# Half 1's x staged in one go, its roots spread together, the sums of x on one engine and the roots one stretch later, in a hybrid attention and retention kernel

## The chip, the cores and the metric

One core of a Trainium2 chip runs the whole program. The metric is the device time of one execution in microseconds; the number given for a kernel is the median of its runs.

## The reference

One layer of a streaming encoder, for 2048 frames of a new stream (the prompt) and 64 frames of a running one (the sample), all in fp32. Every frame is normalised and goes through one wide projection; its columns are the inputs of a differential attention and of a retention, with gates; both results are projected, merged by the gates, projected again and added to x.

```python
h = rmsnorm(x, norm_g) @ w_in                     # 1024 -> 6144
qa, ka, va, za, qb, kb, vb, zb, ga, gb = split(h)
qa, ka = rmsnorm(qa, qn_g), rmsnorm(ka, kn_g)
oa = diff_attention(qa, ka, va, lam, slopes)      # 4 heads, block-causal, ALiBi
ob = retention(qb, kb * 128 ** -0.5, vb, log_g)   # 4 heads, chunks of 64
oa = rmsnorm(oa, subln_g) * 0.2 * silu(za)
ob = rmsnorm(ob) * silu(zb)
y = x + (sigmoid(ga + b0) * (oa @ w_oa) + sigmoid(gb + b1) * (ob @ w_ob)) @ w_out
```

`rmsnorm` divides each row by the root of its mean square plus 1e-6. The sample's attention also reads 4096 cached keys and values. The normalised keys, the values and the final retention states are outputs too.

## The kernel before

Every fp32 factor is split in a high part of type fp32r and the rest (`hi`, `lo`, or `xh`/`xl` and `wh`/`wl`), and a product is three matmuls: high by high, high by rest, rest by high. The high part is an ACT copy, the rest a subtraction on DVE or POOL.

**The work** is written by a planner in Python. Generators (tasks) emit instructions and yield a time or a condition; the loop runs the task of the lowest priority number whose time has come. The planner keeps a clock for each engine (`self.pe`, `self.act`, `self.dve`, `self.pool`, and `self.dma` for loads) and adds an estimate for each instruction. Buffers are counted by tags: `take` waits for one, `give` returns it with the time from which it is free; `either` takes from the tag that is free first. `self.ar` is an arena of columns, 7104 wide until the prompt's attention starts: `grab` takes stretches of it, `drop` returns them. PE, ACT and DVE execute in the order in which the tasks emit. The instructions of POOL and the DMA issues, all of them on SP, are put in order by the framework.

**The order.** The projection runs as a stream of weight columns (`w_stream`, priority 9) over half 0 (frames 0 to 1023 and the sample), then over half 1 (1024 to 2047). x of a half lies transposed in SBUF as `xh` and `xl`, in two segments of 512 frames. Half 0 begins with three groups of columns in natural layout, va, k and q (`natural`; 128 frames and 512 columns a bank, banks `mm`, of which there are two), then vb (`late`: the second segment first), then q, k of the retention and the gates by Strassen products of seven instead of eight (`strassen`): their left factors are blocks of x and sums of blocks, S1, S2, S4 and a third that replaces a block. `x_sums` (priority 1) forms the sums. For each of four c it adds `xh` and `xl` of two blocks again (`pool_sum` on POOL, L735; `raw_sum` on DVE, L739), adds or subtracts and splits the result (`s_split`, L753 and L756). S1 is formed in the stretch of k, S2, S4 and the third from the end of q on, when their room is free; the third goes back into segment 1 of x once vb has read it.

**The sample's attention** (`sample_attn`, priority 4) starts when the sample's q, k and v are stored, and is woven into half 0's products. It holds 2816 columns of the arena (`held`) and up to four stretches of 1024 for scores. At its end four small matmuls by `fold` (L1768) form its output, the held columns are dropped, and `rms_t` normalises it with the bank `tp`, of which there is one, and one buffer each of `ath` and `atl` (two exist).

**Half 1's x** is normalised in two steps. `x_roots` (spawned after k) loads each of the eight tiles of 128 frames into a stretch of 1024, and `x_root` squares and sums it on ACT (L402), with a reciprocal root on ACT and DVE (L406 to L416); the eight results are columns of `self.roots`. After the first unit of gb, three units before half 0 ends, `x_scaled` and `x_split` start. `x_stage` loads x transposed, in four parts of 256 frames, each two tiles of 128 x 1024: parts 0, 1 and 3 in the arena, part 2 in the two `V` buffers, which the sample uses for its values. For each part `x_scaled` multiplies the unit matrix by the roots (DVE, L449), spreads them over all partitions by matmuls with a matrix of ones (L457, bank `tp`), copies the bank (ACT, L460) and scales x by them and by the norm's gain (DVE, L467, eight of 128 x 256). `x_split` waits until half 0 has read a segment for the last time (`seg_free`, set in the last Strassen unit), and splits each part: four copies on ACT (L499) and four subtractions on DVE (L501).

**The passage.** Half 1 starts with va's first 256 columns: four groups of 256 frames, each of which needs its part's split (`xt_ready`). A group ends in `fin_va`: ACT copies the bank to `thi` (L1245) and `ev` (L1247), DVE subtracts into `tlo` (L1249), and three stores follow. There is one `thi` buffer, there are two of `tlo` and three of `ev`. k and q go through `fin_qk`, with transposes (L1201) into `tp` and `thi` again (L1211 or L1216). `attn_zone` waits until half 0 is done and all eight `xt_ready` are there; it closes the pool that held arena, `V`, `S` and `ath`, opens the attention's pool in its place, and loads at once `dnear`, the keys (`K`), queries (`q`), `dfar` and values (`V`) of two heads and the retention's tables and first blocks, 32 DMAs. The attention of half 0's frames then runs at a higher priority than half 1's projection: scores (L1514, L1515, banks `s` and `tp`), their evacuation on DVE (L1523), the exponential on ACT (L1554), and so on.

Of the kernel before, what the change touches and what calls it, by code (L numbers as in the profile page):

```python
# [8 lines left out]
F32 = mybir.dt.float32  # L9
# [3 lines left out]
ALU = mybir.AluOpType  # L13
# [28 lines left out]
PACE = 700.0  # L42
# [93 lines left out]
class Hybrid:  # L136
# [283 lines left out]

    def x_stage(self):
        for p in range(4):
            if p == 2:
                yield from self.take("V", 2)
                xT = [self.sb(self.ap, [128, 1024], "V", "xT") for _ in range(2)]
            else:
                xT = [span.ap for span in (yield from self.stage(p))]
            t0 = 1024 + 256 * p
            for k in range(2):
                tx = self.ld(xT[k].rearrange("p (c t) -> p c t", c=4),  # L430
                             self.i["x_prompt_T"][512 * k:512 * k + 512, t0:t0 + 256]
                             .rearrange("(c p) t -> p c t", p=128), 1 << 19)
            self.xstaged.append((xT, tx))
            yield self.pe

    def x_scaled(self):


        nc = self.nc
        self.xstaged = []  # L440
        self.spawn(self.x_stage(), 1, "w")
        for p in range(4):
            yield lambda: len(self.xstaged) > p
            xT, tx = self.xstaged[p]
            span = yield from self.grab(256)
            dp = span.ap
            yield lambda: len(self.rooted) >= 8
            for u in range(2):
                nc.vector.tensor_scalar(dp[:, 128 * u:128 * u + 128], self.ident,  # L449
                                        self.roots[:, 2 * p + u:2 * p + u + 1], None, op0=ALU.mult)  # L450
                t = self.V(128, self.pe)
            yield max(t, tx)
            yield from self.take("tp")
            rb = self.psum("tp")[:, :256]
            for u in range(2):
                usl = slice(128 * u, 128 * u + 128)
                nc.tensor.matmul(rb[:, usl], self.ones, dp[:, usl], start=True, stop=True)  # L457
                t = self.P(512)
            yield t
            nc.scalar.copy(dp, rb)  # L460
            t = self.A(256, t)
            self.give("tp", t)
            yield t
            for k in range(2):
                for c in range(4):
                    xc = xT[k][:, 256 * c:256 * c + 256]
                    nc.vector.scalar_tensor_tensor(out=xc, in0=xc, scalar=self.gT[:, 4 * k + c:4 * k + c + 1],  # L467
                                                   in1=dp, op0=ALU.mult, op1=ALU.mult)
                    t = self.V(300, t)
                    yield self.dve - PACE  # L470
            self.xscaled.append((xT, t))
            self.drop(span, t)

    def stage(self, p):
        self.staged[p] = yield from self.grab(1024, 1024)
# [2 lines left out]
    def x_split(self):  # L478
        nc = self.nc
        for p in range(4):  # L480
            seg, col = p // 2, 256 * (p % 2)
            yield lambda: len(self.xscaled) > p
            xT, t = self.xscaled[p]
            if p % 2 == 0:
                yield lambda: self.seg_free[seg] is not None
                yield self.seg_free[seg]
                self.seg_free[seg] = None
                self.x_alloc(seg)
                if seg:
                    for k, x in enumerate((self.xh, self.xl)):  # L490
                        ts = self.ld(x[1][:, :, 512:576].bitcast(F32), self.xkeep[:, :, 64 * k:64 * k + 64], 1 << 18)
            yield t
            for k in range(2):
                for c in range(0, 4, 2):
                    ks = slice(4 * k + c, 4 * k + c + 2)
                    hi = self.xh[seg][:, ks, col:col + 256]
                    lo = self.xl[seg][:, ks, col:col + 256]
                    xk = xT[k][:, 256 * c:256 * c + 512].rearrange("p (c t) -> p c t", c=2)
                    nc.scalar.copy(hi, xk)  # L499
                    t2 = self.A(512, self.pe)  # L500
                    nc.vector.tensor_sub(lo, xk, hi.bitcast(F32))  # L501
                    t2 = self.V(612, t2)
                if p == 2:
                    self.give("V", t2)
                else:
                    self.drop(self.staged[p][k], t2)
                yield self.act - PACE
            self.xt_ready += [t2, t2]
# [222 lines left out]
                self.give(r[3], t, 3)  # L731
        yield self.pe

    def pool_sum(self, out, h, l):
        self.nc.gpsimd.tensor_add(out, h.bitcast(F32), l.bitcast(F32))  # L735
        self.tpool = self.G(512, self.pe)

    def raw_sum(self, out, h, l, t):
        self.nc.vector.tensor_add(out, h.bitcast(F32), l.bitcast(F32))  # L739
        return self.V(512, t)  # L740
# [22 lines left out]
    def x_sums(self):  # L763
        nc = self.nc
        yield lambda: len(self.xt_ready) > 8
        yield self.xt_ready[8]
        yield from self.s_room("S1")
        (a11, a12, a21, a22) = (self.x_block(k) for k in range(4))
        for c in range(4):
            r = yield from self.grab(1024)  # L770
            r0, r1 = r[:, 0:512], r[:, 512:1024]
            self.raw_sum(r0, a21[0][:, c], a21[1][:, c], self.pe)
            self.pool_sum(r1, a22[0][:, c], a22[1][:, c])
            yield self.tpool
            nc.vector.tensor_add(r0, r0, r1)
            t = self.V(512)
            yield from self.s_split("S1", c, r0, t)
            self.drop(r, self.dve + LAT)
        yield from self.s_room("S2")
        yield from self.s_room("S4")  # L780
        third, r, r2 = yield from self.grab(2048, 1024, 1024)
        for c in range(4):
            r0, r1, r3, r4 = r[:, 0:512], r[:, 512:1024], r2[:, 0:512], r2[:, 512:1024]
            d = third[:, 512 * c:512 * c + 512]
            self.pool_sum(r1, a11[0][:, c], a11[1][:, c])
            t1 = self.tpool
            self.pool_sum(r4, a21[0][:, c], a21[1][:, c])
            self.raw_sum(r0, *(s[c // 2][:, c % 2] for s in self.S["S1"]), self.pe)
            self.raw_sum(r3, a12[0][:, c], a12[1][:, c], self.pe)
            yield t1  # L790
            nc.vector.tensor_sub(r0, r0, r1)
            t = self.V(512)
            nc.vector.tensor_sub(r3, r3, r0)
            t2 = self.V(512)
            yield from self.s_split("S2", c, r0, t)
            yield from self.s_split("S4", c, r3, t2)
            yield self.tpool
            nc.vector.tensor_sub(d, r1, r4)
            t3 = self.V(512)
            yield self.dve - PACE  # L800
        self.formed = self.dve + LAT
        self.drop(r, self.formed)
        self.drop(r2, self.formed)
        yield lambda: self.seg1_read is not None
        yield max(t3, self.seg1_read)
        done = []
        for c in range(4):
            nc.scalar.copy(a21[0][:, c], third[:, 512 * c:512 * c + 512])
            done.append(self.A(512, self.pe))
        for c in range(4):  # L810
            yield done[c]
            nc.vector.tensor_sub(a21[1][:, c], third[:, 512 * c:512 * c + 512], a21[0][:, c].bitcast(F32))
            self.s3_ready = self.V(512, done[c])
        self.drop(third, self.s3_ready)
        self.summed = True
# [841 lines left out]
    def sample_attn(self):  # L1657
        nc = self.nc
# [108 lines left out]
        for h in range(4):  # L1767
            nc.tensor.matmul(fp[:, 64 * h:64 * h + 64], oall[:, 128 * h:128 * h + 128], self.fold[:, :64],  # L1768
                             start=True, stop=True)
            t = self.P(512)  # L1770
        for span in held:
            self.drop(span, t)
        o, leave = yield from self.rms_t(fp, 256, self.gsub, t, "pv")
        for h in range(4):
            t = self.put(self.oaT[h], o[:, 64 * h:64 * h + 64], T, 64, True)
# [817 lines left out]
    def w_stream(self):  # L2593
# [51 lines left out]
        for half in range(2):  # L2645
            for k, (c0, f, *_) in enumerate(seqs[half]):
                if c0 is None:
                    self.spawn(self.mark(f"{f}{half}"), 0)
                else:
                    yield from f(half)  # L2650
                if half == 0 and k == 1:
                    self.spawn(self.x_roots(), 2, "w")
                if half == 0 and k == len(seqs[0]) - 1:
                    self.done.add("half0")
                    self.marks["half0"] = self.pe
                if half == 0 and k == len(seqs[0]) - 4:
                    self.xt_ready = []
                    self.spawn(self.x_scaled(), 1, "w")
                    self.spawn(self.x_split(), 1, "w")
# [165 lines left out]
```

## Time and profile before

| what | value |
|---|---|
| median of three runs | 1930.66 us (1928.85 to 1931.25) |
| the profiled execution's own time | 1928.47 us |
| its span, first to last instruction | 1926.5 us |
| mean granted TensorE clock | 0.994 of full speed |
| busy: PE, DVE, ACT, POOL | 98%, 67%, 49%, 31% |

The profile is one execution; its page gives busy times, costliest groups and DMA queues, and its trace answers questions by line, tile or stretch of time. In the timeline a row is start, duration, engine, line, operation, output and inputs, and, in brackets, the idle time before it and what ended it. A busy PE is not PE at its peak, since matmuls overlap; the granted clock tells when it ran at half rate.

### The profile page before, as it was taken

What the parts mean: (1) busy time and instruction counts of PE and PEld (TensorE: products, weight loads), DVE (VectorE), ACT (ScalarE), POOL (GpSimd) and SP (SyncE); (2) the same over time, 40 slices, a digit from 0 to 9 for tenths busy, and PEclk for the clock granted to TensorE, in tenths of its full rate; (3) what the DMA queues carried; (4) which work ended last, traced back from release to release, by engine and by line L of the source; (5) the groups of instructions that cost most, each with busy time, mean ns of one, the idle gap of its engine ahead of it and who ended that gap; (6) DMA issues with size and microseconds to landing.
All of it is one profiled execution on the core that took longest, in us unless ns stands there. A gap on an engine that the chain in (4) does not pass through costs nothing. (4 is left out here: it accounts for less than half of the span.)

```text
span 1926.5 us, 33600 instructions
## 1 busy us (share of the span) xinstructions
PE 1896.9 (98%) x11690; PEld 1696.0 (88%) x11690; DVE 1283.2 (67%) x3046; ACT 949.6 (49%) x2153; POOL 598.7 (31%) x569
## 2 busy tenths in 40 slices
PE   9999999999998999999999999999999999999999
PEld 7777888888877999999999899999999999999887
DVE  6666656665655688856576655558677359997664
ACT  6444445454433456555455555456556455554221
POOL 2520455555652111211211112120211245532442
PEclk9999999999999999999999999999999999999999
DMA  7664356565645867454433643362441488886542
GB/s 249 211 211 131 115 159 189 173 172 172 201 146 167 243 178 210 136 162 136 133 101 108 190 113 103 107 160 84 126 114 38 138 245 261 250 250 209 181 153 77
DMA packets 361323, 313.10 MB, mean 163 GB/s; under 512 B 67905, under 2 KB 319937, under 8 KB 361154
## 3 DMA queue, kind: packets, MB, share of 16 engines
q1 hardware_dynamic: 361154, 310.97, 55.0%
q8 instruction: 92, 1.51, 0.3%
q14 instruction: 77, 0.63, 0.1%
HBM read 205.43 MB, written 104.60 MB: 161 GB/s over the span
## 5 line engine op out<-in xcount | busy, mean ns | idle before, releaser
L961 POOL TENSOR_TENSOR wl<-ws,wh 128x512 fp32r<-128x512 f32 x125 | 171.8, 1387 | 412.8 <-ACT wh L951 326.2
L997 PE MATMUL mm<-xh,wh 128*128 128x512 f32 (+2 forms) x768 | 257.3, 335 | 0.0
L997 PE MATMUL mm<-wh,xh 128*128 128x256 f32 (+1 forms) x760 | 251.4, 331 | 4.7 <-ACT raw L1166 3.0
L997 PE MATMUL mm<-xh,wl 128*128 128x512 f32 (+2 forms) x768 | 251.6, 328 | 0.0
L997 PE MATMUL mm<-xl,wh 128*128 128x512 f32 (+2 forms) x768 | 251.5, 327 | 0.0
L997 PE MATMUL mm<-wh,xl 128*128 128x256 f32 (+1 forms) x760 | 245.2, 323 | 0.3 <-DVE xl L501 0.3
L997 PE MATMUL mm<-wl,xh 128*128 128x256 f32 (+1 forms) x760 | 244.7, 322 | 0.0
L1641 DVE TENSOR_TENSOR atl<-at,ath 128x512 fp32r<-128x512 f32 (+1 forms) x144 | 93.9, 660 | 126.4 <-ACT ath L1639 125.5
L997 PEld LDWEIGHTS mm<-wh,xh 128*128 128x128 f32 x760 | 147.2, 194 | 16.5 <-ACT raw L1166 3.6
L1554 ACT ACTIVATE row<-row,a_mx 128x896 f32<-128x896 f32 (+5 forms) x144 | 149.5, 1041 | 19.6 <-DVE a_mx L1533 19.4
L997 PEld LDWEIGHTS mm<-wl,xh 128*128 128x128 f32 x760 | 147.3, 194 | 10.9
L997 PEld LDWEIGHTS mm<-wh,xl 128*128 128x128 f32 x760 | 146.6, 193 | 11.4 <-DVE xl L501 0.5
L997 PEld LDWEIGHTS mm<-xh,wh 128*128 128x128 f32 x768 | 145.0, 189 | 10.7
L997 PEld LDWEIGHTS mm<-xl,wh 128*128 128x128 f32 x768 | 145.2, 189 | 10.3
L997 PEld LDWEIGHTS mm<-xh,wl 128*128 128x128 f32 x768 | 144.8, 189 | 10.6
L1639 ACT CAST ath<-at 128x512 fp32r<-128x512 f32 (+1 forms) x144 | 79.6, 563 | 138.0 <-PE at L1626 136.0
L1523 DVE CUSTOM_DVE_ANT_0 row<-s,dfar 128x512 f32<-128x512 f32 (+2 forms) x146 | 90.5, 636 | 44.9 <-PE s L1515 38.4
L1398 POOL TENSOR_TENSOR r_y<-r_y,r_sq 128x256 f32<-128x256 f32 x32 | 26.8, 838 | 298.0 <-DVE r_sq L1395 173.1
L1514 PE MATMUL s<-K,q 128*128 128x512 f32 (+3 forms) x242 | 91.6, 380 | 7.0 <-DMA q<-qT 5.2
L1576 DVE SCALAR_TENSOR_TENSOR row<-row,a_w 128x896 f32<-128x896 f32 (+6 forms) x88 | 97.5, 1121 | 0.0
L951 ACT CAST wh<-ws 128x512 fp32r<-128x512 f32 x128 | 77.2, 619 | 35.2 <-PE mm L997 15.9
L721 POOL TENSOR_TENSOR wl<-ws,wh 128x256 fp32r<-128x256 f32 x64 | 55.3, 864 | 121.8 <-ACT wh L712 113.7
(489 smaller groups left out, 5475.5 us busy)
## 6 DMA issues: line engine op xcount, KB each, us to landing
ws<-in_w_in_dram SPq DMA_DIRECT2D x160, 256.0 KB, 3.3
q<-qT SPq DMA_DIRECT2D x128, 128.0 KB, 3.8
K<-kT SPq DMA_DIRECT2D x48, 256.0 KB, 4.2
V<-vN SPq DMA_DIRECT2D x24, 512.0 KB, 5.2
row<-in_x_prompt_dram SPq DMA_DIRECT2D x16, 512.0 KB, 5.0
wz<-in_w_in_dram SPq DMA_DIRECT2D x32, 256.0 KB, 4.6
row<-in_cache_k_T_dram SPq DMA_DIRECT2D x32, 256.0 KB, 3.4
row<-in_cache_v_diff_dram SPq DMA_DIRECT2D x32, 256.0 KB, 3.4
```

The costliest lines, as they stand in the source:

```text
L721: nc.gpsimd.tensor_sub(l[:, cs], src, h[:, cs].bitcast(F32))
L951: self.nc.scalar.copy(h, st)
L961: self.nc.gpsimd.tensor_sub(l, st, h.bitcast(F32))
L997: nc.tensor.matmul(ps, p, q, start=c == 0 and i == 0, stop=c == KC - 1 and i == 2)
L1398: nc.gpsimd.tensor_mul(y, y, sq)
L1514: nc.tensor.matmul(ps, q1s, kk, start=True, stop=False)
L1523: nc.vector.tensor_tensor_reduce(out=row[:, k0:k0 + n], in0=ps, in1=tab, scale=-SLOPES[h], scalar=3.0e38, op0=ALU.add, op1=ALU.min, accum_ ...
L1554: nc.scalar.activation(u, u, AF.Exp, bias=mx, scale=-1.0, accum_out=lp[:, k:k + 1])
L1576: nc.vector.scalar_tensor_tensor(out=u0, in0=u1, scalar=w[:, 0:1], in1=u0, op0=ALU.mult, op1=ALU.add)
L1639: nc.scalar.copy(ah[:, :w], at[:, :w])
L1641: nc.vector.tensor_sub(al[:, :w], at[:, :w], ah[:, :w].bitcast(F32))
```

## The change

Four edits:

- **Staging.** Part 0 goes into the two `V` buffers; parts 1 to 3 go into the arena, and wait for `n_spv == 5`, which is set when the sample's last matmuls are emitted and its held columns dropped.
- **Spreading.** `x_scaled` spreads the roots before the loop over the parts: twice 512 columns, in the two `ath` buffers, through whichever of the banks `at`, `tp`, `pv` is free first. The parts then read slices of them.
- **Sums.** `pool_sum` is gone; all sums of `xh` and `xl` are on DVE, and the order inside an iteration changes a little.
- **Roots.** `x_roots` is spawned after q instead of after k.

```diff
 def x_stage(self):
     for p in range(4):
-        if p == 2:
+        if p == 0:
             yield from self.take("V", 2)
             xT = [self.sb(self.ap, [128, 1024], "V", "xT") for _ in range(2)]
         else:
+            yield lambda: self.n_spv == 5
             xT = [span.ap for span in (yield from self.stage(p))]
...
 def x_scaled(self):
...
+    yield lambda: len(self.rooted) >= 8 and self.n_spv == 5
+    rows = []
+    for i in range(2):
+        yield from self.take("ath")
+        rows.append(self.sb(self.ap, [128, 512], "ath", "rb"))
+        for u in range(4):
+            nc.vector.tensor_scalar(rows[i][:, 128 * u:128 * u + 128], self.ident,
+                                    self.roots[:, 4 * i + u:4 * i + u + 1], None, op0=ALU.mult)
+            t = self.V(128, self.pe)
+        yield t
+        bank = yield from self.either(1, "at", "tp", "pv")
+        rb = self.psum(bank)
+        for u in range(4):
+            usl = slice(128 * u, 128 * u + 128)
+            nc.tensor.matmul(rb[:, usl], self.ones, rows[i][:, usl], start=True, stop=True)
+            t = self.P(512)
+        yield t
+        nc.scalar.copy(rows[i], rb)
+        t = self.A(512, t)
+        self.give(bank, t)
     for p in range(4):
         yield lambda: len(self.xstaged) > p
         xT, tx = self.xstaged[p]
-        span = yield from self.grab(256)
-        dp = span.ap
-        yield lambda: len(self.rooted) >= 8
-+        dp = rows[p // 2][:, 256 * (p % 2):256 * (p % 2) + 256]
         yield max(t, tx)
...
 def x_sums(self):
...
-            self.pool_sum(r1, a22[0][:, c], a22[1][:, c])
-            yield self.tpool
+            self.raw_sum(r1, a22[0][:, c], a22[1][:, c], self.pe)
+            yield self.dve - PACE
...
-            self.pool_sum(r1, a11[0][:, c], a11[1][:, c])
-            t1 = self.tpool
-            self.pool_sum(r4, a21[0][:, c], a21[1][:, c])
+            self.raw_sum(r1, a11[0][:, c], a11[1][:, c], self.pe)
             self.raw_sum(r0, *(s[c // 2][:, c % 2] for s in self.S["S1"]), self.pe)
+            yield self.dve - PACE
             self.raw_sum(r3, a12[0][:, c], a12[1][:, c], self.pe)
-            yield t1
...
-            yield self.tpool
+            self.raw_sum(r4, a21[0][:, c], a21[1][:, c], self.pe)
+            yield self.dve - PACE
             nc.vector.tensor_sub(d, r1, r4)
...
 def sample_attn(self):
...
         for span in held:
             self.drop(span, t)
+        self.n_spv = 5
         o, leave = yield from self.rms_t(fp, 256, self.gsub, t, "pv")
...
 def w_stream(self):
...
-                if half == 0 and k == 1:
+                if half == 0 and k == 2:
                     self.spawn(self.x_roots(), 2, "w")
```

In `x_split` the `V` buffers are returned after part 0 instead of part 2, and `ath` is returned after parts 1 and 3.

More of the change, by code (lines that the diff above doesn't have):

```diff
@@ L444, in x_scaled @@
             xT, tx = self.xstaged[p]
-            span = yield from self.grab(256)
-            dp = span.ap
-            yield lambda: len(self.rooted) >= 8
[L448 to L451, printed above, removed]
-            yield max(t, tx)
[L453 to L463, printed above, removed]
+            dp = rows[p // 2][:, 256 * (p % 2):256 * (p % 2) + 256]
+            yield max(t, tx)
             for k in range(2):
@@ L471, in x_scaled @@
             self.xscaled.append((xT, t))
-            self.drop(span, t)
+            if p % 2:
+                self.give("ath", t)
     def stage(self, p):
@@ L502, in x_split @@
                     t2 = self.V(612, t2)
-                if p == 2:
+                if p == 0:
                     self.give("V", t2)
@@ L732, in sum_low @@
         yield self.pe
-    def pool_sum(self, out, h, l):
-        self.nc.gpsimd.tensor_add(out, h.bitcast(F32), l.bitcast(F32))
-        self.tpool = self.G(512, self.pe)
     def raw_sum(self, out, h, l, t):
```

## The prediction

> **What bounds the kernel now.** I read the page first: which engine is busy, and how much of the span is left over.
>
> ```profile
> span 1926.5 us, 33600 instructions
> PE 1896.9 (98%) x11690; PEld 1696.0 (88%) x11690; DVE 1283.2 (67%) x3046; ACT 949.6 (49%) x2153; POOL 598.7 (31%) x569
> ```
>
> TensorE is the bound. The change takes no matmul away, so it can win only PE's 29.6 us of idle time and what the slow clock costs after a gap, and it can lose only by making new gaps. So the next view is the waits of PE (in total, times, longest), and then a table of windows around them: the window's length, PE's busy time first and, after POOL's, the granted clock, the DMA share and GB/s.
>
> ```profile
> PE s L1514 <- DMA q<-qT: 5.2, 2, 4.2
> PE tp L1201 <- DVE raw L1186: 3.3, 2, 2.2
> PE mm L997 <- ACT raw L1166: 3.0, 2, 1.9
> PE tp L1372 <- DVE r_hi L1364: 2.9, 1, 2.9
> ...
> PE mm L997 <- ACT xh L499: 1.7, 1, 1.7
> ...
> PE tp L847 <- DVE row L1390: 1.2, 1, 1.2
> ```
>
> ```profile
> 80.00:90.00 10.00, 7.84 (x31) 6.02 (x30) 9.76 (x17) 3.77 (x9) 3.86 (x3) 0.83 0.67 179
> 140.00:150.00 10.00, 8.06 (x30) 5.89 (x29) 6.58 (x23) 5.20 (x15) 0.47 (x1) 0.83 0.42 118
> 610.00:620.00 10.00, 8.01 (x52) 7.61 (x52) 3.10 (x5) 4.39 (x8) 0.66 (x1) 0.83 0.59 168
> 620.00:632.00 12.00, 7.32 (x37) 6.99 (x37) 2.98 (x12) 4.07 (x12) 3.10 (x3) 0.72 1.12 255
> 648.00:656.00 8.00, 5.11 (x31) 4.82 (x31) 4.01 (x10) 4.14 (x12) 2.79 (x2) 0.79 1.04 291
> ```
>
> Idle time plus the missing clock gives each window's loss. At 80: 2.2 + 1.7 = 3.9 us. At 140: 1.9 + 1.7 = 3.6. At 610: 2.0 + 1.7 = 3.7. At 620: 4.7 idle, and of the 0.28 × 12 = 3.4 of clock some 2.6 outside the idle time, 7.3. At 648: 2.9 + 1.5 = 4.4. The first two belong to the sums of x and to the roots, the last three to the passage from half 0 to half 1, 15.4 us together. The change touches all five.
>
> **Part 1: the sums of x leave POOL.** The stall at 82 to 85 is a chain of small DVE multiplies that PE's transposes wait for. Rows of DVE, then of POOL:
>
> ```profile
> 81.45 1.21 DVE L338 TENSOR_TENSOR sm_t<-sm_t,ms 128x8 f32<-128x8 f32 x1
> ...
> 89.11 0.17 DVE L338 TENSOR_TENSOR sm_t<-sm_t,ms 128x8 f32<-128x8 f32 x1
> ```
>
> ```profile
> 81.36 1.28 POOL L735 TENSOR_TENSOR row<-xh,xl 128x512 f32<-128x512 f32 x1
> ```
>
> The same multiply takes 0.17 us alone and 1.21 us beside POOL's sum: it ends when the sum ends. Without L735 the low half of a weight (L961) that follows it on POOL moves up by 1.28 us and blocks the same chain, so one block of about 1.2 us goes and one stays. The gap of 2.2 becomes some 1.0, and whether the clock still falls after that I leave even: between 0 (a new sum on DVE ahead of the chain takes the place of the block) and 3.9 us won. I take 1.2 and half of the 1.7, 2.
>
> [...]
>
> What the twelve sums cost on DVE, by both lines (ns, min/median/max):
>
> ```profile
> L735 POOL TENSOR_TENSOR row<-xh,xl x12: 1282/1296/1736, 55.2 to 208.9; 128x512 f32<-128x512 f32 x12
> L739 DVE TENSOR_TENSOR row<-xh,xl x8: 676/684/1787, 66.3 to 207.7; 128x512 f32<-128x512 f32 x8
> ```
>
> 12 × 0.68 = 8.2 us more on DVE over 150 us, against 12 × 1.30 = 15.6 us less of POOL, beside which DVE's sums grew to 1.79. No wait of PE falls between 150 and 230, where two thirds of these sums run, so they are hidden by PE's own products. If that cover goes, the first product that reads the sums is late by no more than these 8.2 us; I count 0.
>
> **Part 2: the roots move from the stretch of q to that of vb.** The stall at 141 to 143 is ACT's:
>
> ```profile
> 140.53 1.05 ACT L402 ACTIVATE row<-row 128x1024 f32<-128x1024 f32 x1
> ...
> 142.62 0.58 ACT L1166 COPY raw<-mm 128x512 f32<-128x512 f32 x1
> ```
>
> A root's square and its small followers hold ACT for 1.6 us (140.53 until L1163 at 142.14); behind them stands the copy that frees PE's bank. Without them the copy ends 1.6 us sooner and 0.3 of the 1.9 us stays: 1.6 won, and the 1.7 of clock. I take 3.3, bounds 0 and 3.6. In the stretch of vb a group's end asks one copy of ACT instead of two passes, so 1.6 us there fits. Eight loads of 512 KB and a room of 1024 columns move along, and share the arena with the sums' 4096 and the sample's 2816: 7936 of 7104. One has to wait, and I expect the sample, whose first scores need 1024 more and so wait for the sums' room already. Its end has 20 us of cover (part 3); without that, its delay would be half 1's.
>
> [...]
>
> **Part 3: half 1's x.** Before, the fourth part's load waits for room, its scaling runs until 609.5, and its split ends at 615.3. DVE's rows, ACT's, and the start of half 1 on PE:
>
> ```profile
> 588.37 1.28 DVE L501 TENSOR_TENSOR xl<-row,xh 128x512 fp32r<-128x512 f32 x2
> ...
> 607.11 2.46 DVE L467 SCALAR_TENSOR_TENSOR row<-row,gT 128x256 f32<-128x256 f32 x6
> ...
> 612.82 2.49 DVE L501 TENSOR_TENSOR xl<-row,xh 128x512 fp32r<-128x512 f32 x4
> ```
>
> ```profile
> 585.90 4.26 ACT L499 CAST xh<-row 128x512 fp32r<-128x512 f32 x8
> ```
>
> ```profile
> 533.27 1.00 PE L1768 MATMUL pv<-fold,row 128*128 128x64 f32 x8
> ```
>
> ```profile
> 593.20 0.28 PE L997 MATMUL mm<-wh,xh 128*128 128x256 f32 x1
> ```
>
> After, the room is free when the sample's fold is done, 533 to 534. Four parts of 1 MB at the 255 GB/s of the window at 620 take 16 us, 32 scalings of 0.41 (2.46 for 6) another 13, partly beside them: all done by some 565, where the splits cannot start before 585.9. So scaling has 20 us of cover; without it half 1 starts late by what is missing. The matmuls that spread the roots stay as many, their copies on ACT go from four of 256 columns to two of 512: nothing, under the same cover. The eight multiplies by the roots now fall into the sample's last norm, where PE already waits 1.2 us (L847, for `tp`): eight at up to 0.41 in front of that norm could double the gap and bring the clock down, 0 to 1.2 + 1.7 lost; I take 0.5, since DVE waits there itself.
>
> The 16 splits now run in one row: ACT 16 × 0.53 = 8.5 us from 585.9, DVE 16 × 0.62 (2.49 for 4) and four evacuations of the last unit, as long, 12.4 us from 586.5. So x is complete at about 599 instead of 615.3. The stall at 610.9 goes: 3.7 us won.
>
> **What is late next.** The attention's pool opens with the last split, and at that instant SP is given all its first loads. SP's rows, then ACT's:
>
> ```profile
> 615.37 0.35 SPq L234 DMA_DIRECT2D dnear<-in_c_dnear_dram  x1
> ...
> 644.91 0.41 SPq L239 DMA_DIRECT2D vN<-thi  x1
> ```
>
> ```profile
> 605.39 0.59 ACT L1245 CAST thi<-mm 128x512 fp32r<-128x512 f32 x1 [2.54 <-PE mm L997]
> ...
> 620.87 0.59 ACT L1245 CAST thi<-mm 128x512 fp32r<-128x512 f32 x1 [0.18 <-PE mm L997]
> ...
> 650.61 0.58 ACT L1216 CAST thi<-tp 128x512 fp32r<-128x512 f32 x1 [5.43 <-DMA vN<-thi]
> ```
>
> The `thi` filled at 620.87 was stored only at 644.91: 32 loads stood ahead of it, 29.5 us from `dnear` on, at a DMA share above 1 (windows at 620 and 648). `thi` has one buffer, so the next user waited until 650.6, and the 2.9 us stall at 650 is that. It was cheap because the pool opened after three of va's four groups. Two groups take from 593.20 to 605.39, so the first is evacuated at 599.3; now the pool opens before that, and the first group's store stands behind the loads: issued at 599 + 29.5 = 628.5, landed 5.7 later (644.91 to 650.61), 634.2. Group 2's `thi` copy, due at 605.4, waits for that; ACT and DVE are in order, and all behind waits too. With its 0.59 and DVE's subtraction after it the bank is free at 635.4. PE has two `mm` banks: it can do groups 1 to 3 (6 us each) and some 4 us of scores (an estimate: half of PE's 7.3 busy us from 620 to 632), 22 us of work in the 42.2 since 593.2: 20 lost. If the scores' evacuations stand behind group 2's on DVE, PE stops at its fourth score in group 3, with 14 us done: 28 lost. I take 25, plus 1.7 of slow clock, 26.7. It replaces all of the 15.4.
>
> Sum: -2 - 3.3 + 0.5 + (26.7 - 15.4) = **+6.5 us**. The profiled execution took 1928.47 us, its span and 2.0 around it; the median shown is 2.2 higher. On the median 1930.66 + 6.5 = 1937.2; I say 1937. With the sum's ends (early savings 0 to 7.5, the norm 0 to 2.9, the jam 20 to 28 with 1.7) it lies between 1929 and 1948.
>
> **Rivals.** (a) The store passes the loads. For it: SP's order is not the program's; `row<-in_x_prompt_T_dram` loads are issued long before their scaling. Then group 2 goes through, group 3's `thi` jams instead, and PE stops one group later: 22 + 6 = 28 us of work in the 42.2, 14.2 lost and 1.7 of clock, 0.5 above the 15.4: -4.3 us in all, 1926.4. (b) The passage closes up: loads 16 us sooner hide the q wait, no jam: -15.4 - 4.8 = -20.2, 1910.5. Against it: the 29.5 us behind `dnear` are bandwidth, and a store must follow in any order. (c) Slower by another mechanism: the 32 scalings follow each other at 540 to 560, and beside POOL a DVE sum grew by 1.1 us (0.68 to 1.79). POOL is busy 31% of the time: 32 × 1.1 × 0.31 = 11 us that DVE falls behind, and half 0's products wait for banks from the point where that is more than a product's time. Some 6 us on top of (a): 1932. Against it: the scalings of before ran beside POOL too, without a wait of PE. (d) The change doesn't do what it says: the fourth part is still late because the arena is cut up; then only parts 1 and 2 and the norm count, -4.8, 1925.9.
>
> **How the numbers follow.** The jam 0.60, (a) 0.16, (b) 0.09, (c) 0.07, (d) 0.08. A measurement here can tell about 0.2%, 3.9 us, from no change. Slower by more: most of the jam's share (0.50) and some of (c), 0.53 with it. Faster by more: (b), (d), 0.09 of (a)'s 0.16, 0.26. The rest, 0.21, is the same. The range leaves out (b) and the top end: 1922 to 1946. The jam's own range is 1929 to 1948.
>
> **What would show it.** Right: `dnear` near 599, the store of the first va group some 29 us behind it, ACT's second `thi` cast waiting on DMA for over 20 us, one PE gap of 15 to 25 us before 636, and no gap at 82 or 141 above 1.2. Wrong: stores between the K loads, or `dnear` still behind 610; or x not scaled by 585.

## The result and the profile after

No change that can be told: 1929.54 us in the median (1925.91 to 1934.36) against 1929.17 (1923.43 to 1932.25) for the kernel before, a ratio of 1.0005 (95% interval 0.9994 to 1.0016). The forecast was 6.5 us slower, with a range from 1922 to 1946; the time lies in the range, but the slowing that was forecast is not there. The profiled execution took 1932.02, 2.5 above its median, so a second profile of the same kernel was taken (below).

The page of the changed kernel, then the waits of PE (in total, times, longest):

```profile
span 1929.9 us, 33596 instructions
PE 1887.0 (98%) x11690; PEld 1689.4 (88%) x11690; DVE 1291.6 (67%) x3058; ACT 947.8 (49%) x2151; POOL 587.9 (30%) x557
```

```profile
PE s L1514 <- DVE a_acc L1523: 25.7, 1, 25.7
PE at L2303 <- DVE ogl L2259: 3.8, 3, 1.8
...
PE tp L1201 <- DVE raw L1186: 0.8, 1, 0.8
...
PE tp L847 <- DVE row L1390: 0.4, 1, 0.4
```

PE is busy 9.9 us less than before for the same 11690 matmuls, most of it slow clock that is gone (at half clock it was busy for 22.2 us before, and for 5.1 now). It is idle 13.3 us more (42.9 against 29.6): one new wait of 25.7 us, with most of the old ones gone. The windows, in the columns that the prediction used, say where:

```profile
80.00:90.00 10.00, 9.21 (x42) 7.15 (x41) 9.79 (x19) 2.87 (x8) 2.16 (x2) 1.00 0.55 157
140.00:150.00 10.00, 10.00 (x49) 8.17 (x48) 4.96 (x14) 3.98 (x11) 0.00 (x0) 1.00 0.32 79
...
606.00:632.00 26.00, 0.67 (x6) 0.46 (x4) 0.56 (x1) 1.59 (x3) 1.26 (x1) 0.58 0.98 254
632.00:640.00 8.00, 7.61 (x39) 7.22 (x40) 5.17 (x24) 6.00 (x19) 3.84 (x3) 0.66 0.70 212
```

At 80 a loss of 0.8 is left of 3.9, at 140 none of 3.6. Between 606 and 632 every engine stands nearly still while the DMA share is 0.98. That is the jam. PE's first product of half 1 and the two ends of the gap:

```profile
584.23 0.28 PE L997 MATMUL mm<-wh,xh 128*128 128x256 f32 x1
...
606.03 0.28 PE L1515 MATMUL tp<-K,q 128*128 128x256 f32 x1
632.39 0.58 PE L1514 MATMUL s<-K,q 128*128 128x256 f32 x1 [25.72 <-DVE a_acc L1523]
```

Half 1 starts at 584.23 instead of 593.20, 9.0 us earlier. From there to the end of the span it takes 1345.7 instead of 1333.3, 12.4 more. The small change is two large ones with opposite signs. What holds the gap, on SP and on ACT:

```profile
590.86 0.37 SPq L239 DMA_DIRECT2D vN<-thi  x1
...
594.91 0.34 SPq L234 DMA_DIRECT2D dnear<-in_c_dnear_dram  x1
...
625.06 0.38 SPq L239 DMA_DIRECT2D vN<-thi  x1
```

```profile
595.99 0.59 ACT L1245 CAST thi<-mm 128x512 fp32r<-128x512 f32 x1 [2.60 <-PE mm L997]
...
630.34 0.59 ACT L1245 CAST thi<-mm 128x512 fp32r<-128x512 f32 x1 [33.27 <-DMA vN<-thi]
```

The `thi` filled at 595.99 is stored only at 625.06, 30.15 us after `dnear`, and the next cast waits 33.27 us for its landing. Between `dnear` and that store SP's rows count 30 loads, `dnear` included: 22 for the two heads and 8 for the retention. The text ahead of the prediction and the prediction itself say 32. DVE sat idle for 33.65 us as well; its rows behind that cast:

```profile
631.44 0.69 DVE L1249 TENSOR_TENSOR tlo<-mm,thi 128x512 fp32r<-128x512 f32 x1 [33.65 <-ACT raw L1247]
632.05 0.28 DVE L1523 CUSTOM_DVE_ANT_0 row<-s,dnear 128x128 f32<-128x128 f32 x1
```

The evacuation of the first scores (L1523, from 632.05) stands behind the subtraction that needs the cast (631.44), so PE stops at its fourth pair of scores.

### The profile page after: what moved, and what is told of

Read it like the earlier page. It is cut to its first block, busy times and chain, and to the rows that moved or that the text cites. A ratio compares the mean times of both kernels' runs of the same rounds, so it can differ in the third digit from the quotient of the medians.

```text
span 1929.9 us, 33596 instructions
## 1 busy us (share of the span) xinstructions
PE 1887.0 (98%) x11690; PEld 1689.4 (88%) x11690; DVE 1291.6 (67%) x3058; ACT 947.8 (49%) x2151; POOL 587.9 (30%) x557
## 4 chain that ended last, share of the span: by engine, by line
PE 89%; DVE 3%; DMA 3%; SPq 1%; issue 1%; ACT 1%; POOL 0%; DVEq 0%; ACTq 0%; POOLq 0%
PE mm L997 35%; PE mm L847 9%; PE tp L847 4%; PE at L1626 3%; PE s L1514 2%; PE s L1515 2%; PE s L847 2%; PE pv L1606 2%; PE pv L1605 2%; PE pv L1604 2%; PE s L2426 1%; PE s L2428 1%; PE s L2427 1%; SPq L234 1%; PE pv L1891 1%
## 5 line engine op out<-in xcount | busy, mean ns | idle before, releaser
L961 POOL TENSOR_TENSOR wl<-ws,wh 128x512 fp32r<-128x512 f32 x125 | 169.8, 1374 | 325.4 <-ACT wh L951 218.3
L1514 PE MATMUL s<-K,q 128*128 128x512 f32 (+3 forms) x242 | 91.7, 380 | 26.4 <-DVE a_acc L1523 25.7
L1523 DVE CUSTOM_DVE_ANT_0 row<-s,dfar 128x512 f32<-128x512 f32 (+2 forms) x144 | 88.9, 629 | 41.9 <-PE s L1515 41.8
```

Of the source, the lines that this page charges most:

```text
L961: self.nc.gpsimd.tensor_sub(l, st, h.bitcast(F32))
L1514: nc.tensor.matmul(ps, q1s, kk, start=True, stop=False)
L1523: nc.vector.tensor_tensor_reduce(out=row[:, k0:k0 + n], in0=ps, in1=tab, scale=-SLOPES[h], scalar=3.0e38, op0=ALU.add, op1=ALU.min, accum_ ...
```

## The experiments

Each kernel was timed beside the kernel before on the same chip. "Start" is PE's first product of half 1, "rest" the span behind it, both in the profiled execution; before has 593.2 and 1333.3.

| kernel | median us | ratio to before (95%) | start | rest |
|---|---|---|---|---|
| changed kernel | 1929.54 | 1.0005 (0.9994 to 1.0016) | 584.2 | 1345.7 |
| the same again | 1929.19 | 1.0005 (0.9994 to 1.0016) | 584.3 | 1339.2 |
| part 1 | 1918.40 | 0.9951 (0.9939 to 0.9963) | 585.1 | 1332.4 |
| part 2 | 1928.73 | 0.9998 (0.9986 to 1.0009) | 594.2 | 1336.4 |
| parts 1 and 2 | 1918.74 | 0.9945 (0.9926 to 0.9963) | 583.3 | 1333.9 |
| parts 1 and 3 | 1927.64 | 1.0003 (0.9993 to 1.0013) | 584.6 | 1340.9 |
| pool late | 1915.40 | 0.9933 (0.9918 to 0.9948) | 585.7 | 1328.1 |
| loads behind | 1917.89 | 0.9943 (0.9923 to 0.9963) | 583.9 | 1327.6 |
| V behind | 1912.24 | 0.9922 (0.9903 to 0.9941) | 583.9 | 1324.2 |
| two stores first | 1913.42 | 0.9932 (0.9917 to 0.9948) | 583.9 | 1326.6 |
| part 1, loads behind | 1925.96 | 0.9980 (0.9969 to 0.9991) | 583.3 | 1339.4 |
| pool late, loads behind k | 1900.13 | 0.9856 (0.9839 to 0.9872) | 583.9 | 1317.1 |
| the same with the old staging of x | 1906.60 | 0.9889 (0.9868 to 0.9909) | 583.0 | 1316.2 |

My theory from the trace: the early stalls are worth more than forecast, the jam about as much as forecast, and they cancel. The rivals: the early gain does not reach the end (transfers, not TensorE, set the passage to half 1), or the gap is bandwidth and not order.

### Parts 1 and 2 without part 3

Before, with the new `x_sums` and

```
-                if half == 0 and k == 1:
+                if half == 0 and k == 2:
                     self.spawn(self.x_roots(), 2, "w")
```

> Parts 1 and 2 alone on the kernel before; x is staged as before. The trace of the changed kernel puts the early savings at 7.9 us by window (3.1 at 82, 1.2 at 121, 3.6 at 141). Theory (early savings and a jam of stores behind loads that nearly cancel each other): nothing behind them eats these, so half 1 starts near 585.3 and the kernel takes 7.9 less than before, some 1921 (ratio 0.9959). Rival (the early savings do not reach the end, since the fourth part's split in the passage is held by transfers and not by TensorE): the stall at 611 grows by what was won, and the time stays within 2 us of before, 1927 to 1931.

Measured: 1918.74, 9.8 less than before beside it. The passage took no part of it: rest 1333.9 against 1333.3. So the first rival falls, and part 3, put on top of these two, takes back some 12 us (0.9945 to 1.0005).

### Part 1 alone

Before with the new `x_sums`, of which one line pair of six:

```
-            self.pool_sum(r1, a22[0][:, c], a22[1][:, c])
-            yield self.tpool
+            self.raw_sum(r1, a22[0][:, c], a22[1][:, c], self.pe)
+            yield self.dve - PACE
```

> Part 1 alone on the kernel before: the twelve sums on DVE. By the prediction 2 us won; by the windows of the changed kernel 3.1 (the gap at 82 to 85 and its slow clock), and 4.3 if the 1.2 us stall at 121 is of its making too: a ratio of 0.9978 to 0.9984, and the stall at 141 to 143 with its slow clock stays. Rival (the sums on DVE cost what they save, and all that parts 1 and 2 won together, 9.8, is the roots'): within 1 us of before.

Measured: 9.7 us won, all that both parts won together. Neither expectation holds. All of PE's waits from 78 to 200 in this kernel:

```profile
PE tp L1200 <- DVE raw L1185: 1.4, 1, 1.4
```

The stalls at 121 and 141 are gone, with the roots where they were. So the roots alone did not make the stall at 141.

At 82 two sums on DVE now stand ahead of the chain of small multiplies, and they are what is slow beside POOL's low halves of a weight (L960, 80.03 to 83.03):

```profile
80.08 3.51 DVE L739 TENSOR_TENSOR row<-xh,xl 128x512 f32<-128x512 f32 x2
...
83.70 0.17 DVE L338 TENSOR_TENSOR sm_t<-sm_t,ms 128x8 f32<-128x8 f32 x1
```

The two take 3.51 us instead of some 1.4 (2 × 0.684, the median before), and the multiply that took 1.21 takes 0.17. PE still waits 1.4 of the 2.2 us, but the granted clock is 1.00 from 80 to 90, where it was 0.83 before.

At 121 no sum on POOL was in the way: in the kernel before, POOL runs none between 82.6 and 185.7. What ran there were low halves of a weight (L961), with DVE's multiply beside them:

```profile
119.68 4.23 POOL L961 TENSOR_TENSOR wl<-ws,wh 128x512 fp32r<-128x512 f32 x3 [35.82 <-ACT wh L951]
```

```profile
121.04 1.73 DVE L1186 TENSOR_TENSOR raw<-raw,sm_y 128x512 f32<-128x512 f32 x1
```

In the kernel with part 1 the halves start at 116.73, and this multiply takes 0.69.

### Part 2 alone

Before with the two-line edit of the roots.

> Part 2 alone on the kernel before: the roots in the stretch of vb, the sums still half on POOL. Part 1 alone won 9.7 us and took away the stalls at 82, 121 and 141, the last of which the prediction gave to the roots. Theory A (the prediction's: a root's square stands ahead of the copy that frees PE's bank, and moving it frees the bank as well): the stall at 141 with its clock goes, those at 82 and 121 stay: 3.6 won, 1924.6 from 1928.2 (1923 to 1926.5). Theory B (what made those stalls was the order that the sums on POOL gave to ACT and DVE behind them; the roots were only what happened to stand there): within 1.5 us of before, 1926.7 to 1930.

Measured: no change (0.9998); theory B's number came true. The window at 140, and ACT in it:

```profile
140.00:150.00 10.00, 7.54 (x35) 5.56 (x34) 5.84 (x16) 4.19 (x11) 0.00 (x0) 1.00 0.26 67
```

```profile
140.11 0.69 ACT L1211 ACTIVATE thi<-tp,gq 128x512 fp32r<-128x512 f32 x1 [6.25 <-PE tp L1201]
140.69 0.62 ACT L1163 ACTIVATE sq<-up 64x512 f32<-64x512 f32 x1
142.80 0.60 ACT L1163 ACTIVATE sq<-mm 128x512 f32<-128x512 f32 x1 [1.49 <-DVE ms L1174]
143.29 0.58 ACT L1166 COPY raw<-mm 128x512 f32<-128x512 f32 x1
```

No root's square is left there, ACT sits idle for 6.25 us, and the copy that frees PE's bank comes at 143.29 all the same, 0.7 later than before. It stands in ACT's order behind the cast of q's transposes (L1211), which waits for PE, and behind a square (L1163) that waits 1.49 us for DVE. That square needs one of the two `tlo` buffers, and DVE frees one when it has reduced the square before (L1174); the reduction stands behind a subtraction (L1212) that needs the same cast. The kernel before has the same pair:

```profile
141.34 0.67 DVE L1174 TENSOR_REDUCE ms<-sq 64x8 f32<-64x512 f32 x1
```

```profile
142.14 0.58 ACT L1163 ACTIVATE sq<-mm 128x512 f32<-128x512 f32 x1
```

DVE ends there at 142.01 and the square starts at 142.14. So the root's square held ACT while ACT had to wait anyway: without it the copy could come 0.13 us sooner, not 1.6.

In the kernel with part 1 alone the same lines, one number lower, stand the other way round:

```profile
132.82 1.06 ACT L402 ACTIVATE row<-row 128x1024 f32<-128x1024 f32 x1 [1.22 <-DMA row<-in_x_prompt_dram]
...
134.44 0.58 ACT L1162 ACTIVATE sq<-mm 128x512 f32<-128x512 f32 x1
134.92 0.58 ACT L1165 COPY raw<-mm 128x512 f32<-128x512 f32 x1
...
138.75 0.69 ACT L1210 ACTIVATE thi<-tp,gq 128x512 fp32r<-128x512 f32 x1 [1.31 <-PE tp L1200]
```

The copy is ahead of the cast, with a root's square (L402) in front of it, and PE does not wait. What part 1 changed at 121 and 141 is when and in which order the engines do this work; that it does so through the finishing times that the kernel's planner reckons for the sums is argued from the code, not shown.

### Parts 1 and 3

The changed kernel with the roots back at `k == 1`.

> Parts 1 and 3: the changed kernel with the roots back in the stretch of q. Theory (the parts add up): the stall at 141 with its clock comes back, 3.6 us (4.8 if the one at 121 is the roots'), half 1 starts at 588 to 589, the gap of 25 us stays as it hangs on when x is complete after half 1's start: 1933 to 1934. Rival (the roots and the sample share the arena, so moving them also moves the sample and x): a gap or a start of half 1 that differs by more than 5 us from that.

Measured: 1.0003, the same as with the roots moved; no stall at 141. So with part 1 in place the roots may stand in either stretch. Its gap is split in two, as the first scores also wait for q:

```profile
PE s L1514 <- DVE a_acc L1523: 21.9, 1, 21.9
PE s L1514 <- DMA q<-qT: 4.1, 1, 4.1
```

Part 3 alone, with the sums left on POOL, was not tried.

### The changed kernel again

> The changed kernel once more, unaltered, for a second profile of it, since its first profiled execution took 2.5 us more than its median while that of before took 0.7 less. Theory (the gap is set by the order of the loads): half 1 starts at 584 again, the gap is 25 to 27 us again and the passage to the end 1344 to 1346; the time lies between 1926 and 1932. Rival (the gap varies with the transfers, and its first profile showed a long one): a gap of 22 us or less in a run of 1927.

Measured: 1929.19 in the median, the profiled execution 1925.62. The start is the same, the gap 22.9 and the rest 1339.2, 6.5 shorter than in the first profile: between the two expectations. PE's gap, and SP's rows:

```profile
PE s L1514 <- DVE a_acc L1523: 22.9, 1, 22.9
```

```profile
595.00 0.35 SPq L234 DMA_DIRECT2D dnear<-in_c_dnear_dram  x1
...
622.16 0.38 SPq L239 DMA_DIRECT2D vN<-thi  x1
```

The same 30 loads took 27.2 us instead of 30.15, and the gap is 2.8 shorter. The order makes the gap; how fast the loads pass sets its length. The other 3.7 us of the 6.5 were not followed.

### The pool late

A counter at the end of `fin_va`, and a condition:

```
+            self.nva += 1024 <= t0 < T
...
-        yield lambda: "half0" in self.done and self.live["r"] == 0 and len(self.xt_ready) == 8
+        yield lambda: "half0" in self.done and self.live["r"] == 0 and len(self.xt_ready) == 8 and self.nva >= 4
```

> The changed kernel, but the attention's pool opens only when all four groups of the first va have emitted their stores (some 609 instead of 595). Theory (the 25.7 us gap is the thi store behind the pool's 32 loads): the gap goes; what comes is a wait of the first score for q like that of before (4.7) and a thi wait of up to 3, with slow clock 8 to 14 us together instead of 27: 1913 (1910 to 1918). Rival (the 7.9 MB of loads have to pass before TensorE can go on, wherever they are put): the gap only moves by 14 us, 1927 or more.

Measured: 1915.40, as the theory says, by another way than it says. There is no wait for q, but ACT and then PE wait later:

```profile
ACT thi L1216 <- DMA kT<-thi: 15.1, 1, 15.1
```

```profile
PE at L1627 <- DVE row L1577: 11.4, 1, 11.4
```

The four stores of va pass (SP takes `dnear` and K between them, from 596.39 on, and all the rest behind them), and the store of k's first `thi` is now behind the last 14 loads. The jam has moved, and costs less, since PE has scores to do by then.

### The later loads behind va's stores

The pool opens early; the second head and the retention wait:

```
             yield from self.head_in(half, h)
+            if h:
+                yield lambda: self.nva >= 4
             yield from self.load_head(half, h)
...
-        yield lambda: "kqv00" in self.done
+        yield lambda: "kqv00" in self.done and self.nva >= 4
         yield from self.ret_some(0, 8)
```

> The changed kernel; the pool opens as early as in it, but the second head's K and V and the retention's tables are asked for only when the fourth group of the first va has emitted its stores. Ahead of the second group's store then stand 4 MB, 14 us, instead of 29.5. Theory: the gap falls from 25.7 to 2 to 6 us and the first scores find their q: 1908 (1904 to 1914). Rival (bandwidth, not order): the loads put off make the gap later, 1925 or more.

Measured: 1917.89. The direction is the theory's; the gap is larger than it said, and the time beyond its range. K, q, `dfar` and V still stand ahead of the store:

```profile
ACT thi L1245 <- DMA vN<-thi: 16.9, 1, 16.9
```

```profile
PE s L1517 <- DVE a_acc L1526: 9.3, 1, 9.3
```

### V behind too

As above, and in `load_head`, ahead of V's loads:

```
+        yield lambda: self.nva >= 3
         for u in range(nu):
...
                 yield from self.take("V")
```

> As the kernel with the loads behind, and the first head's V too waits until the third group has emitted its stores. 1 MB less stands ahead of the store of the second group, 3.5 us. Theory: the gap falls to 0 to 3 us, 1906 (1903 to 1912), if V's later landing holds up no product; if it does, the same as the kernel with V ahead. Rival (bandwidth): 1925 or more.

Measured: 1912.24, just beyond the theory's range. ACT's cast and PE's gap:

```profile
609.12 0.58 ACT L1245 CAST thi<-mm 128x512 fp32r<-128x512 f32 x1 [12.40 <-DMA vN<-thi]
```

```profile
PE s L1518 <- DVE a_acc L1527: 4.9, 1, 4.9
```

With the changed kernel this makes a row of three with the same cast and three amounts of loads ahead of it: it waits 33.3, 16.9 and 12.4 us, and PE's gap is 25.7, 9.3 and 4.9. The difference is 7.6, 7.6 and 7.5: PE has 7.5 us of work without that cast, and every further microsecond of its wait is lost.

### Two stores first

As V behind, and the pool opens at `self.nva >= 2`.

> As the kernel with V behind, and the pool opens only when the second group of the first va has emitted its stores, so that its thi store stands ahead of K and q instead of 9.3 us behind them. Theory: the third cast of thi, which waited 12.4 us there, waits under 3; the stall of 4.9 us at the first scores becomes 0 to 2, and K and q come 2 to 3 us later, which may hold the first score for as long: 1909 (1905 to 1912), from 1912. Rival (the first scores are bound by when K and q land, and the order ahead of them no longer matters): 1912 to 1915.

Measured: 1913.42, no better than V behind. The third cast does not wait for DMA, as expected, and the fourth does:

```profile
601.33 0.59 ACT L1245 CAST thi<-mm 128x512 fp32r<-128x512 f32 x1 [4.64 <-PE mm L997]
...
613.35 0.59 ACT L1245 CAST thi<-mm 128x512 fp32r<-128x512 f32 x1 [6.42 <-DMA vN<-thi]
```

```profile
PE s L1518 <- DVE a_acc L1527: 5.8, 2, 5.5
```

The rival's number came true for another reason than it gave. The store let past moved the jam to the next user of `thi`.

### Part 1 with the later loads behind va's stores

The kernel with part 1 alone, and the edit of the later loads.

> Part 1 alone (x staged as before, 1918.4), with the second head's and the retention's loads behind the fourth group's stores. Theory: the thi wait of 2.7 us at 641 with its slow clock goes, 4 us; the wait for q (7.8) and for x's fourth part (3.4) stay: 1914.5 (1912.5 to 1916.5), so that x staged early is worth 2 us once the stores are not behind (1912.2 for the kernel with V behind). Rival (x staged early is what the rest of the gain hangs on): 1917 or more.

Measured: 1925.96, a ratio of 0.9980 where part 1 alone has 0.9951. The rival's number (1917 or more) came true; neither side gave the reason. The wait at 641 went and came back larger, at k:

```profile
ACT thi L1215 <- DMA kT<-thi: 8.3, 1, 8.3
```

```profile
PE tp L1516 <- DVE tlo L1216: 6.2, 1, 6.2
...
PE s L2304 <- DVE ogl L2260: 2.7, 1, 2.7
PE at L2304 <- DVE ogl L2260: 2.6, 2, 1.7
```

The last two lie in the output stage at the end, where part 1 alone lost 0.8. Their sum differs from kernel to kernel, and why stays open.

### Pool late, loads behind k

As the pool late, with a second counter in `fin_qk` (`self.nk += which == "k" and 1024 <= t0 < T`), and the second head and the retention wait for `self.nk >= 4`.

> As the kernel whose pool opens after four stores (1915.4), and the second head's K and V and the retention's tables wait until the first k too has emitted its four stores. In that kernel one gap of 11.4 us was left at 635 to 646: ACT's cast of k's thi waited 15.1 us on a store behind these 16 loads. Theory (order): the gap goes with its slow clock, 12 to 13 us, and 1 to 2 come back where the late loads are waited for: 1904 (1901 to 1908). Rival (the retention or the second head is late by what the loads are put off, 14 us or more): 1913 or more.

Measured: 1900.13, a ratio of 0.9856 (0.9839 to 0.9872), 3.9 better than expected. The window of the old gap:

```profile
606.00:632.00 26.00, 25.34 (x204) 24.83 (x204) 14.53 (x50) 10.93 (x30) 4.67 (x4) 1.00 0.89 261
```

261 GB/s now flow beside a PE that is busy for 25.34 of 26 us; in the changed kernel it was 254 beside 0.67. So the bytes that flowed were not what stopped PE there; the order was. This version beats both kernels.

### The same with the old staging of x

Parts 1 and 2 with all the conditions of the last kernel.

> The fastest kernel (pool after four stores of va, the rest of its loads after four stores of k; 1900.1) with x staged as before; sums and roots as in the changed kernel. The question is what part 3 is worth once no store stands behind a load. Theory: the split of x's fourth part holds TensorE as before (1.7 + 0.3 idle at the split and its slow clock, 3.7) and the room of the pool comes some 11 us later, so that the first score waits for q (5 to 8): 1907 to 1912. Rival (order is everything, and early staging gives nothing): 1899 to 1902.

Measured: 1906.60, 0.9889 (0.9868 to 0.9909), just below the theory's 1907. In the passage PE waits for the split as expected, and little for q:

```profile
PE mm L996 <- ACT xh L499: 1.7, 1, 1.7
PE s L1517 <- DMA q<-qT: 1.0, 1, 1.0
```

So early staging may be worth some 6 us once the order is mended, but the two intervals overlap a little, and the profiled executions do not show it: this one took 1901.04 and the last kernel's 1902.94, of which PE's waits in the output stage are 0.2 here and 4.3 there.

## Why the prediction was wrong

**Part 1, -2 forecast, -8 to -10 measured.** This is the step that failed, and with it the term for the early savings in the sum. "One block of about 1.2 us goes and one stays" is not what happened at 82: in part 1 alone the small multiply is as short as elsewhere (0.17 us at 83.70), and the new sums ahead of it are slow (3.51 for two). That 1.4 us of idle stays, and the granted clock stays at 1.00, gives 2.5 us: near the forecast 2, by another way, which is luck. The rest of the gain was put at nothing or elsewhere. The second wait in the row quoted for this part ("3.3, 2, 2.2"), 1.1 us at 121, was not priced; the stall at 141, 3.6 with its clock, was given to part 2; and PE's wait at the sample's norm, 1.2, goes with part 1 as well. These four make 8.4 us, and half 1 starts 8.1 us earlier in that kernel. Why the norm's wait goes was not followed.

**Part 2, -3.3 forecast, 0 measured.** "Without them the copy ends 1.6 us sooner" read the instruction in front of the copy as its cause. With the square taken out the copy is as late, since the square ahead of it waits for DVE; with it left in, another order is early. That 7936 columns do not fit in 7104 cost PE nothing that shows here.

**Part 3, the norm.** +0.5 forecast; the wait at the norm is 0.4 with all three parts, and it is none with part 1 alone, parts 1 and 2, or parts 1 and 3. So its fall from 1.2 is not part 3's, and against those kernels the 0.5 is near. The scaling was not done by 565:

```profile
L471 DVE SCALAR_TENSOR_TENSOR row<-row,gT,rb x24: 472/480/1527, 560.2 to 592.0; 128x256 f32<-128x256 f32 x24
```

It ended at 592, among half 0's own work and the splits of the earlier parts on DVE, and the last split at 594.8. By the prediction's own sign that is wrong, and the 20 us of cover were not enough: the splits began at 576.6 instead of 585.9, so that by the forecast's own 12.4 us x could have been complete near 590. That the pool still opened near the forecast 599 is luck: half 0's earlier end and the late scaling nearly cancel.

**What is late next, +11.3 forecast.** Right in mechanism and near in size: 12.4 in the first profile, 5.9 in the second, 10 to 12 between the medians with and without part 3 (0.9951 to 1.0003, 0.9945 to 1.0005). The gap was 25.7 and 22.9 for 25, which was a value between the two ways that I gave for PE to stop; it is the one at the fourth score. It lies one group later than I had it (the second store, the third cast), because the pool opened 10.7 us behind half 1's first product and not 5.8.

**The sum.** -4.8 and +11.3 were forecast, some -10 and +11 measured, so that the forecast slowing did not come. Against rival (b) I held that the loads are bandwidth and a store must follow them in any order; the kernel at 1900, below that rival's 1910.5, shows that it need not.

The clock is the smaller lesson. The slow stretches of three profiles are multiples of 3.41 us (last section), and at a granted clock of 0.50 one of 3.41 costs 1.7. A gap of 1.9 us at 141 before had one behind it, a gap of 2.46 us there with part 2 alone had none, so by these runs the likely price of such a gap lies between none and 1.7; the prediction took the 1.7 at 141 whole.

## What to carry to other kernels

Two stalls under one row of the waits are two prices. The instruction in front of a late one in an engine's order is not yet its cause: look for what else the late one would wait for, and take the suspect out alone before giving the stall to it. A tile with one buffer was stored here through the queue that also takes prefetches, and opening the room for the prefetches earlier put the store behind 30 of them, 30.15 us. In such a case ask for each load only when the stores that free such tiles are out (1900.13 here, against 1929.54), and follow the jam to the tile's next user: letting one store past only moved it (the fourth cast waited 6.42 us).

## What the runs showed of the hardware

In the kernel before the granted clock was 0.50 in five stretches of 3.41 us and one of 6.83, in the changed kernel in one of 27.31, and in its second profile in one of some 24, added up from the clock of its windows (the stretch that the span's end cuts off is left out): once, twice, eight and seven times 3.41. In the kernel before, gaps of 2.2 us at 82, 1.9 at 141 and 2.9 at 650 were each followed by a stretch of 3.41, and so were two of 1.7 and 0.3 close together at 611 and two of 1.0 and 1.1 at 852; a gap of 4.2 at 622 came before the stretch of 6.83. But 1.4 us at 82 in the kernel with part 1 alone and 2.46 us at 140 in the kernel with part 2 alone were not followed by one (granted clock 1.00 in both windows). The same 30 loads took 27.2 and 30.15 us in two executions of the same kernel.
